# Up-projection of a feed-forward block on one core: 40 of 44 units issued from an explicit timetable, weight differences stored in half one and reloaded in half two

## Chip, cores and metric

One core of a Trainium2 chip. The metric is the device time of one execution of the whole kernel in microseconds, on the slowest core; here there is one. A lower time is better.

## The reference, cut to what matters

The kernel computes one layer of a streaming encoder, x of 2048 tokens x 1024, all in float32: three mixers (mLSTM, RG-LRU, Mamba-2), an output projection, and then a gated feed-forward block with a short causal convolution. The change lies in the first product of that block and what follows it up to the second one:

```
def causal_dwconv(x, w, b):             # K = 3 here
    ...
    for k in range(K):
        out = out + xp[:, k:k + S] * w[k]

def conv_ffn(x, w_up, conv_w, conv_b, w_down):
    u = causal_dwconv(x @ w_up, conv_w, conv_b)     # w_up: 1024 x 5632
    g, v = jnp.split(u, 2, axis=-1)
    return (jax.nn.gelu(g) * v) @ w_down            # w_down: 2816 x 1024

def reference(x, ...):
    ...
        h = rms_norm(x, norm_ffn_pre[l])
        x = x + rms_norm(conv_ffn(h, ...), norm_ffn_post[l])
```

## The kernel before, in words

**Units.** `phase_u` computes the up-projection, the convolution and the gate. It takes the tokens in two halves of 1024 and, in each, the 22 blocks of the feed-forward width (128 channels of the gate g and 128 of the value v): 44 units. Units 0 to 21 are the first half, 22 to 43 the second. Blocks come in pairs: block j, then block 11 + j. In the program's names `u0_14` is block 14 in the first half, and `uw0_15` the weights of block 15; the trace leaves the half and the running number out (`u_14`, `uw_15`). So block 4's unit comes after `u_14` and before `u_15`. "Unit 21" and the like mean the place in the order, counted from 0; "block 4's unit" goes by the name (its place is 8).

**A unit on PE.** A unit is a product [2 x 512 tokens, 1024] x [1024, 2 x 128], done by a Winograd form of 2 x 2 blocks: seven block products in place of eight. Each product is four k-steps (one 128-row slice each), and each k-step is three matmuls of 128 x 128 by 512 (lines 108 to 110: high times high part, high times low, low times high; `split3`), since float32 values are split in a high and a low part. That makes 84 matmuls. The products go b11 to bank X, b21 to Y, T4 to V, T1 to Z, T2 onto X, b22 onto Z, T3 onto X. Between them the banks' partial sums are copied out by ACT (line 356: `p1` of X, `p5` of Z, `u2` and `u3` of X), and DVE adds the copies and banks into the two outputs `ca` (gate channels) and `cb` (value channels) (lines 407, 421, 426, 427). X and Z take a further product after a copy, so that product can't begin before the copy is done.

**A unit's weights**, made in the unit before it (`Product.weights`): two raw tiles `ra`, `rb` are loaded on SP's queue, 512 KB each (four raw buffers in all). DVE makes four differences T1 to T4 (line 138). ACT makes the seven high parts (line 131, rounded copies), POOL the seven low parts (line 133, source minus high part).

**After the products** (`conv`, lines 430 to 447): ACT applies the last tap and the bias, DVE the other two taps for each output (line 438, `scalar_tensor_tensor`). The first two tokens of a half need two tokens of the half before: `ftail` holds them. In the first half DVE copies them there (line 446), in the second two tiny taps per output read them (line 442). ACT then does gelu on the gate channels (line 1740) and DVE the product of gelu and value (line 1741). For the down-projection, which is Winograd too, the block of a pair's first unit is kept, and after the second unit DVE makes four sums of blocks (lines 1634 to 1637). All blocks go to DRAM (`aS`, line 1619, on SP; for unit 42 on POOL's queue). Units 8, 11, 14 and 17 in order also make the sums of the second half's input, and units 20 to 41 one set of differences of the down weights each (lines 97 to 102: three on DVE, one on POOL).

**Ends.** Unit 0 finishes the phase before, unit 21 reloads PE's input blocks for the second half, unit 43 makes the first operands of the down-projection (`down_head`, `d_2l` at line 1785 is one of them). Units 21 and 22 take their products in another order (`sums_first`).

**What orders the work.** All of this is issued under a scheduler that places each engine's instructions by its own estimate of when operands are ready; `tc.high_priority(offset=EVAC)` pulls the copies and additions out of the banks forward.

## Time and profile before

| what | value |
|---|---|
| median of 3 runs | 2752.56 us (2748.34 to 2753.48) |
| profiled execution, its own time | 2752.25 us |
| its span | 2750.5 us |
| mean granted clock of PE | 0.961 |
| PE busy | 2490.6 us, 91% of the span |
| DVE busy | 2136.2 us, 78% |
| ACT busy | 1395.3 us, 51% |
| POOL busy | 1226.4 us, 45% |

The span is 1.75 us shorter than the execution's own time. It holds the mixers, the output projection, the up-projection from about 1270 to 2290 us, and the down-projection after it. Shares are means over all of these; a statement on the up-projection has to be read from its own stretch of time. Engines are named PE (matmuls), DVE, ACT, POOL and SP (issues most transfers). A PE that is shown busy runs at the granted clock: 1.00 is 2.4 GHz, 0.50 is 1.2 GHz.

### The profile page before, as it was taken

How to read it: one execution, taken by the hardware profiler on the slowest of the kernel's cores; microseconds unless marked ns; L12 is line 12 of the kernel's file. 1: busy time of each engine (PE TensorE's matmuls, PEld its weight loads, DVE VectorE, ACT ScalarE, POOL GpSimd, SP SyncE). 2: the span in 40 equal slices, each digit the busy share in tenths (PEclk: the TensorE clock that was granted, in tenths of full speed). 3: DMA queues.
4: the chain of work that ended last, by engine and by line, in shares of the span. 5: the costliest groups of instructions: out<-in, count | busy, mean ns of one | idle time of the engine just before them, and what ended most of it. 6: DMA issues, size and time to landing. Idle time of an engine off the chain costs nothing.

```text
span 2750.5 us, 38721 instructions
## 1 busy us (share of the span) xinstructions
PE 2490.6 (91%) x13658; PEld 2143.4 (78%) x13658; DVE 2136.2 (78%) x3055; ACT 1395.3 (51%) x2392; POOL 1226.4 (45%) x876
## 2 busy tenths in 40 slices
PE   8899989898888899999998989888989898999997
PEld 7677867688888778877776867666767677999997
DVE  5897689857888854556998889998989887557766
ACT  5456554544667765565444434543434356446343
POOL 5554454434344522224765556675555564003222
PEclk9999989999999999999999999999999999999999
DMA  7444633256666554665234333643434338767786
GB/s 244 149 145 144 221 127 118 83 178 184 167 174 179 180 183 146 206 217 172 95 119 139 122 123 111 191 149 119 138 127 138 126 121 304 252 202 267 265 267 206
DMA packets 290323, 467.41 MB, mean 170 GB/s; under 512 B 20832, under 2 KB 195680, under 8 KB 290128
## 3 DMA queue, kind: packets, MB, share of 16 engines
q1 hardware_dynamic: 289056, 461.53, 52.0%
q8 instruction: 107, 1.75, 0.3%
q0 software_dynamic: 784, 2.36, 0.2%
q10 hardware_dynamic: 288, 1.05, 0.1%
q14 instruction: 88, 0.72, 0.1%
HBM read 320.42 MB, written 144.44 MB: 169 GB/s over the span
## 4 chain that ended last, share of the span: by engine, by line
PE 22%; DVE 18%; DMA 8%; issue 5%; ACT 2%; POOL 1%; DVEq 0%; SPq 0%; ACTq 0%; POOLq 0%
PE mix L110 1%; PE mix L109 1%; PE mix L108 1%; PE e_7b L108 1%; PE e_7b L110 1%; PE e_7b L109 1%; DVE us L1634 1%; DMA e_0a<-aS 1%; PE e_2b L110 0%; PE e_2b L108 0%; PE e_2b L109 0%; PE e_6b L110 0%; PE e_6b L108 0%; PE e_6b L109 0%; DMA uw_9rb<-in_wup_u_dram 0%
## 5 line engine op out<-in xcount | busy, mean ns | idle before, releaser
L984 POOL TENSOR_TENSOR yn<-yn,yg 128x512 f32<-128x512 f32 x16 | 22.1, 1382 | 147.3 <-DMA yg<-gate 103.7
L1891 POOL TENSOR_TENSOR o<-o,y 128x512 f32<-128x512 f32 x14 | 24.6, 1757 | 125.7 <-DVE y L1890 25.9
L1785 POOL TENSOR_TENSOR d_0l<-d_0r,d_0h 128x768 fp32r<-128x768 f32 x2 | 3.9, 1942 | 146.8 <-ACT d_0h L1784 146.8
L108 PE MATMUL mix<-wo,ym 128*128 128x512 f32 x128 | 51.9, 405 | 1.6 <-DVE ysl L1015 1.6
L110 PE MATMUL mix<-wo,ym 128*128 128x512 f32 x128 | 51.0, 398 | 0.7 <-DVE ym L1015 0.7
L109 PE MATMUL mix<-wo,ym 128*128 128x512 f32 x128 | 50.6, 395 | 0.0
L109 PE MATMUL mix<-wol,ysh 128*128 128x512 f32 x128 | 50.2, 393 | 0.0
L110 PE MATMUL mix<-woh,ysl 128*128 128x512 f32 x128 | 50.1, 392 | 0.0
L108 PE MATMUL mix<-woh,ysh 128*128 128x512 f32 x128 | 49.7, 393 | 0.0
L1497 DVE TENSOR_TENSOR bh<-hT,g 128x512 f32<-128x512 f32 x32 | 20.7, 685 | 32.1 <-PE hT L1496 24.9
L1015 DVE TENSOR_TENSOR ym<-yT,ym 128x512 fp32r<-128x512 f32 x16 | 11.0, 689 | 35.6 <-ACT ym L1014 35.6
L986 DVE TENSOR_TENSOR yn<-yn,yg 128x1024 f32<-128x1024 f32 x16 | 21.2, 1328 | 18.7 <-ACT yg L985 18.7
L1801 DVE TENSOR_TENSOR e_10l<-e_10a,e_10h 128x896 fp32r<-128x896 f32 x15 | 16.3, 1090 | 23.8 <-ACT e_10h L1800 21.5
L1001 POOL TENSOR_SCALAR yrh<-yr 128x512 fp32r<-128x512 f32 x16 | 11.2, 702 | 51.7 <-DMA yr<-yrT 51.7
L1800 ACT ACTIVATE e_8h<-e_8a 128x896 fp32r<-128x896 f32 x15 | 14.3, 954 | 37.7 <-DMA e_8a<-aS 29.4
L616 DVE TENSOR_TENSOR hT<-xT,par 128x512 f32<-128x512 f32 x32 | 21.4, 683 | 14.7 <-PE xT L615 14.7
L615 PE MATMUL xT<-ident,x 128*128 128x128 f32 x128 | 20.2, 305 | 13.4 <-DVE x L609 8.3
L839 ACT ACTIVATE no<-n 128x256 f32<-128x256 f32 x64 | 23.9, 374 | 16.3 <-PE n L110 7.0
L1486 ACT ACTIVATE bt<-bx 128x1024 f32<-128x1024 f32 x16 | 16.9, 1059 | 27.7 <-DVE bx L1485 27.7
L1801 DVE TENSOR_TENSOR e_9l<-e_9a,e_9h 128x896 fp32r<-128x896 f32 x15 | 16.4, 1091 | 18.3 <-ACT e_9h L1800 16.7
L1801 DVE TENSOR_TENSOR e_6l<-e_6a,e_6h 128x896 fp32r<-128x896 f32 x15 | 23.9, 1590 | 8.0 <-ACT e_6h L1800 8.0
L985 ACT ACT_TABLE_LOAD x16 | 20.5, 1283 | 18.2 <-DMA yg<-gate 18.1
(9711 smaller groups left out, 11524.5 us busy)
## 6 DMA issues: line engine op xcount, KB each, us to landing
x<-in_x_dram SPq DMA_DIRECT2D x16, 512.0 KB, 6.5
hT<-hT SPq DMA_DIRECT2D x16, 512.0 KB, 3.9
gate<-no SPq DMA_DIRECT2D x64, 128.0 KB, 3.0
yn<-yns SPq DMA_DIRECT2D x16, 512.0 KB, 4.8
yg<-gate SPq DMA_DIRECT2D x16, 512.0 KB, 4.6
bx<-in_x_dram SPq DMA_DIRECT2D x16, 512.0 KB, 4.9
x<-bx SPq DMA_DIRECT2D x16, 512.0 KB, 2.8
h2T<-bh SPq DMA_DIRECT2D x16, 512.0 KB, 4.3
```

What stands on the lines that cost most here:

```text
L108: a = nc.tensor.matmul(pss, lh, rh, start=first, stop=False, skip_group_check=True)
L109: nc.tensor.matmul(pss, lh, rl, start=False, stop=False, skip_group_check=True)
L110: nc.tensor.matmul(pss, ll, rh, start=False, stop=last, skip_group_check=True)
L616: nc.vector.tensor_tensor(hT[:, 4 * q : 4 * q + 4], pt.rearrange("p (a b) -> p a b", a=4), col(par, "g1", 4 * q, 4).unsqueeze(2).to_broadc ...
L839: nc.scalar.activation(o, pt[:, 0:256], AF.Copy)
L984: nc.gpsimd.tensor_tensor(yn[:, 512:], yn[:, 512:], g[:, 512:], op=ALU.mult)
L985: nc.scalar.activation(g, g, AF.Sigmoid)
L986: nc.vector.tensor_tensor(yn, yn, g, op=ALU.mult)
L1497: nc.vector.tensor_tensor(hT[:, q * 4 : q * 4 + 4, :], pt.rearrange("p (a b) -> p a b", a=4), g2[:, 4 * q : 4 * q + 4].unsqueeze(2).to_bro ...
L1634: nc.vector.tensor_tensor(c, a11, a21, op=ALU.subtract)
L1801: nc.vector.tensor_tensor(al, a, ah.bitcast(F32), op=ALU.subtract)
L1891: nc.gpsimd.tensor_tensor(o[i][:, hs], o[i][:, hs], t, op=ALU.add)
```

## The change

Units 1 to 20 and 23 to 42 are written as events with a time each, in slots of one k-step (three matmuls), 28 slots a unit, and are then issued in the order of these times within `tc.manual_schedule()`. The four others (0, 21, 22, 43) stay with the scheduler. What is computed stays as it was. Beside the order, the code in the timetable differs in these points:

- The low parts are made by DVE (line 1911), all but one a unit (b11, on POOL).
- In the first half the four differences of each unit are stored in DRAM (`wT`, 4 x 256 KB a unit); in the second half they are loaded from there, seven slots before the end of the unit that stands two before theirs, and not made again.
- `ca` and `cb` have two more columns in front. In the second half ACT copies the tail into them, and each tap is one instruction; in the first half ACT instead of DVE saves the tails (line 1811).
- The taps of `cb` come ahead of those of `ca`.
- Unit 42's blocks are stored from SP's queue. The raw tiles of a unit are asked for two units ahead.

```
-        def weights(self, tp, w_ap, nm, sums_first=False, on_dve=()):
+        def weights(self, tp, w_ap, nm, sums_first=False, on_dve=(), diffs=None, save=None):
...
+            if diffs is not None:
+                T1, T2, T4 = (loaded(i) for i in (0, 1, 3))
+            else:
+                T1 = self.sub(nm + "T1", b12, b11)
...
+            if save is not None:
+                for i, t in enumerate((T1, T2, T3, T4)):
+                    nc.sync.dma_start(save[:, i], t)
...
+        def unit_events(n, at):
...
+            half, pos, b, nm = where(n)
+            t0, t1 = 28 * n, 28 * (n + 1)
...
+                for k in range(4):
+                    at(t0 + 4 * q + k, step, bk, wn, hn, first, k)
...
+            at(t0 + 4, keep, "p1", "X")
+            at(t0 + 9.4, c_of, 0)
+            at(t0 + 9.5, evac, "ca", 0, "Y", "p1")
+            at(t0 + 16, keep, "p5", "Z")
+            at(t0 + 20, keep, "u2", "X")
+            at(t0 + 24.1, c_of, 1)
+            at(t0 + 24.2, evac, "cb", 0, "Z", "u2")
+            at(t1, keep, "u3", "X")
+            at(t1, evac, "cb", 1, "X", "p5")
+            at(t1 + 0.8, evac, "ca", 1, "u3", "V", ALU.subtract)
...
+            at(t1 + 1.0, conv0, 1)
+            at(t1 + 2.8, conv0, 0)
+            if half == 0:
+                at(t1 + 4.6, tails)
+            at(t1 + 4.4, tap, 1, 1)
+            at(t1 + 6.3, tap, 1, 2)
+            at(t1 + 8.3, tap, 0, 1)
+            at(t1 + 10.2, tap, 0, 2)
+            at(t1 + 13, gelu)
+            at(t1 + 15.2, gate)
...
+            if b < NJ:
+                return [(17, keep)]
+            return [(17, store_blocks), (17.2, s3), (18.2, s1), (19.2, s2), (22, s4), (25, store_sums)]
+
+        def weight_events(n, at):
...
+            t0 = 28 * (n - 1)
...
+            at(t0 - 28 + (9 if aux(n - 3) else 2), load)
+            early = 5 if sums_first(n) else 0
+            if half:
+                at(t0 - 28 + 21, load_t)
+            else:
+                at(t0 + 1.7 - early, diff, "T1", "b12", "b11")
+                at(t0 + 2.4 - early, diff, "T2", "b22", "T1")
+                at(t0 + 3.1 - early, diff, "T4", "T2", "b21")
+                at(t0 + 12.2 - 2 * early, diff, "T3", "b22", "b12")
+                at(t0 + 5.1, store_t, 1, 2, 4)
+                at(t0 + 13.1, store_t, 3)
+            names = ("T1", "T2", "b22", "T3", "b11", "T4", "b21") if early else (
+                "b11", "b21", "T4", "T1", "T2", "b22", "T3"
+            )
+            for i, (name, th, tl) in enumerate(zip(
+                names, (-1, 2.5, 5, 7, 11, 15, 19), (0, 4.0, 6.2, 8.2, 12.1, 16.5, 20.2)
+            )):
+                at(t0 + th, hi, name)
+                at(t0 + tl, lo, name, nc.vector if i else nc.gpsimd)
...
+            at(t0 + 17.5, load)
+            at(t0 + 26, make)
+            at(t0 + 28 + 3, store)
...
+            with tc.manual_schedule():
+                for _, _, f, args in sorted(ev, key=lambda e: e[:2]):
+                    f(*args)
...
+        single(0, finish_b)
+        steady(1, NFF - 1)
+        single(NFF - 1, next_half)
+        single(NFF, None)
+        steady(NFF + 1, N - 1)
+        last(W_[N - 1], where(N - 1)[3], 1, where(N - 1)[2])
```

How the order of instructions moves, at three places. First ACT's queue in the first unit of block 4 (`u0_4`; the unit before it is `u0_14`, and `uw0_15` are the weights of the unit after it; `h` ends a high part, `p1`, `p5`, `u3` are copies out of banks, `v14` and `v36` the convolution's outputs). Before:

```order
L131 ACTIVATE uw0_15T4h_13797<-uw0_15T4_13795 128x512
L356 ACTIVATE u0_14u3_13744<-u0_14X_13648 128x512
L435 ACTIVATE u0_14v14_13748<-u0_14ca_13646,upar_12337 128x1024
L356 ACTIVATE u0_4p1_13837<-u0_4X_13821 128x512
L435 ACTIVATE u0_14v36_13753<-u0_14cb_13647,upar_12337 128x1024
L131 ACTIVATE uw0_15T1h_13801<-uw0_15T1_13791 128x512
L131 ACTIVATE uw0_15T2h_13805<-uw0_15T2_13793 128x512
L1740 ACTIVATE u0_14v14_13748<-u0_14v14_13748 128x1024
L131 ACTIVATE uw0_15b22h_13809<-uw0_15rb_13781 128x512
L131 ACTIVATE uw0_15T3h_13815<-uw0_15T3_13813 128x512
L356 ACTIVATE u0_4p5_13876<-u0_4Z_13823 128x512
```

and in the change:

```order
L1908 ACTIVATE uw0_15b21h_13815<-uw0_15ra_13650 128x512
L1801 ACTIVATE u0_14v14_13818<-u0_14ca_13705,upar_12337 128x1024
L1775 ACTIVATE u0_4p1_13829<-u0_4X_13793 128x512
L1811 ACTIVATE ftail_12339<-u0_14ca_13705 128x2
L1811 ACTIVATE ftail_12339<-u0_14cb_13776 128x2
L1908 ACTIVATE uw0_15T4h_13838<-uw0_15T4_13823 128x512
L1908 ACTIVATE uw0_15T1h_13852<-uw0_15T1_13804 128x512
L1908 ACTIVATE uw0_15T2h_13873<-uw0_15T2_13813 128x512
L1814 ACTIVATE u0_14v14_13818<-u0_14v14_13818 128x1024
L1908 ACTIVATE uw0_15b22h_13894<-uw0_15rb_13652 128x512
L1775 ACTIVATE u0_4p5_13901<-u0_4Z_13876 128x512
```

The convolution of `cb` (`v36`) moved ahead of that of `ca` (`v14`), the two copies of the tails came in (L1811), T3's high part moved from ahead of `p5` to behind it, and gelu (L1740 before, L1814 now) still stands ahead of `p5`.

Second, DVE's queue at the same place (`T1` to `T4` are weight differences; a name that ends in `l` is a low part). Before:

```order
L446 COPY ftail_12339<-u0_14cb_13647 128x2
L138 TENSOR_TENSOR uw0_5T1_13950<-uw0_5rb_13940,uw0_5ra_13938 128x512
L446 COPY ftail_12339<-u0_14ca_13646 128x2
L138 TENSOR_TENSOR uw0_5T2_13952<-uw0_5rb_13940,uw0_5T1_13950 128x512
L438 SCALAR_TENSOR_TENSOR u0_14v14_13748<-u0_14ca_13646,upar_12337,u0_14v14_13748 128x1023
L138 TENSOR_TENSOR uw0_5T4_13954<-uw0_5T2_13952,uw0_5ra_13938 128x512
L438 SCALAR_TENSOR_TENSOR u0_14v14_13748<-u0_14ca_13646,upar_12337,u0_14v14_13748 128x1022
L407 TENSOR_TENSOR u0_4ca_13819<-u0_4Y_13822,u0_4p1_13837 128x512
L438 SCALAR_TENSOR_TENSOR u0_14v36_13753<-u0_14cb_13647,upar_12337,u0_14v36_13753 128x1023
```

and in the change:

```order
L1785 TENSOR_TENSOR u0_14ca_13705<-u0_14u3_13790,u0_14V_13696 128x512
L138 TENSOR_TENSOR uw0_15T1_13804<-uw0_15rb_13652,uw0_15ra_13650 128x512
L138 TENSOR_TENSOR uw0_15T2_13813<-uw0_15rb_13652,uw0_15T1_13804 128x512
L138 TENSOR_TENSOR uw0_15T4_13823<-uw0_15T2_13813,uw0_15ra_13650 128x512
L1911 TENSOR_TENSOR uw0_15b21l_13816<-uw0_15ra_13650,uw0_15b21h_13815 128x512
L1743 SCALAR_TENSOR_TENSOR u0_14v36_13799<-u0_14cb_13776,upar_12337,u0_14v36_13799 128x1023
L1911 TENSOR_TENSOR uw0_15T4l_13839<-uw0_15T4_13823,uw0_15T4h_13838 128x512
L1743 SCALAR_TENSOR_TENSOR u0_14v36_13799<-u0_14cb_13776,upar_12337,u0_14v36_13799 128x1022
L1911 TENSOR_TENSOR uw0_15T1l_13853<-uw0_15T1_13804,uw0_15T1h_13852 128x512
L1743 SCALAR_TENSOR_TENSOR u0_14v14_13818<-u0_14ca_13705,upar_12337,u0_14v14_13818 128x1023
L1785 TENSOR_TENSOR u0_4ca_13864<-u0_4Y_13825,u0_4p1_13829 128x512
L1743 SCALAR_TENSOR_TENSOR u0_14v14_13818<-u0_14ca_13705,upar_12337,u0_14v14_13818 128x1022
```

Low parts (L1911) stand between the differences and the taps now, which were on another engine before; the copies of the tails (L446) are gone; the differences are those of the next unit (`uw0_15`), not of the one after (`uw0_5`); the taps of `v36` are ahead of those of `v14`.

Third, POOL's queue at the end of the stage (`aS` is the blocks' array in DRAM, `dl` and `d0_2l` are first operands of the down-projection). Before:

```order
L1608 TENSOR_TENSOR dl0_1_0_19909<-da0_1_19906,dh0_1_0_19908 128x384
L1619 DMA aS_9883<-u1_10v10_19755 128x4x128
L1608 TENSOR_TENSOR dl1_1_0_19919<-da1_1_19916,dh1_1_0_19918 128x384
L1619 DMA aS_9883<-us1_10_0_19978 128x2x128
L1619 DMA aS_9883<-u1_21v21_19770 128x2x256
L1619 DMA aS_9883<-us1_10_2_19989 128x2x128
L1619 DMA aS_9883<-u1_21v21_19770 128x2x256
L1619 DMA aS_9883<-u1_10v10_19755 128x2x128 x4
L1619 DMA aS_9883<-u1_21v21_19770 128x2x128
L1785 TENSOR_TENSOR d0_2l_20140<-d0_2r_20135,d0_2h_20139 128x768
```

and in the change:

```order
L1621 TENSOR_TENSOR dl0_1_0_19964<-da0_1_19961,dh0_1_0_19963 128x384
L1621 TENSOR_TENSOR dl1_1_0_19974<-da1_1_19971,dh1_1_0_19973 128x384
L1632 DMA aS_9883<-us1_10_0_20033 128x2x128
L1632 DMA aS_9883<-us1_10_2_20044 128x2x128
L2084 TENSOR_TENSOR d0_2l_20195<-d0_2r_20190,d0_2h_20194 128x768
L1632 DMA aS_9883<-u1_21v21_19825 128x2x256
```

Unit 42's store (the first row of `u1_10v10`) is gone from this queue, and `d0_2l`, which stood behind all the stores shown, has two of unit 43's ahead of it now; the others follow it.

## Rows read from the trace of the kernel before

**Rows 1.** Windows: first stretch, transition, second; last three columns: clock, DMA share, GB/s.

```profile
1290.00:1731.00 441.00, 404.36 (x1683) 326.37 (x1682) 388.15 (x370) 192.66 (x288) 270.40 (x149) 0.95 0.36 116
1731.00:1784.00 53.00, 41.32 (x169) 32.79 (x169) 50.68 (x51) 27.93 (x45) 35.48 (x21) 0.90 0.66 208
1784.00:2248.70 464.70, 410.66 (x1682) 329.97 (x1682) 410.80 (x438) 188.62 (x285) 263.23 (x164) 0.94 0.41 131
```

**Rows 2.** Timeline of PE (start, duration): first matmuls of blocks 4, 15, 6, 17.

```profile
1437.53 0.40 PE L108 MATMUL u_4X<-uQ_0a11h,uw_4b11h 128*128 128x512 f32 x1
...
1466.31 0.40 PE L108 MATMUL u_15X<-uQ_0a11h,uw_15b11h 128*128 128x512 f32 x1
...
1532.73 0.40 PE L108 MATMUL u_6X<-uQ_0a11h,uw_6b11h 128*128 128x512 f32 x1
...
1552.03 0.40 PE L108 MATMUL u_17X<-uQ_0a11h,uw_17b11h 128*128 128x512 f32 x1
```

**Rows 3.** PE's waits (us, times, longest): the first stretch's longest, the second's.

```profile
PE u_4Z L108 <- ACT u_4p L356: 7.5, 1, 7.5
...
PE u_5Z L108 <- ACT u_5p L356: 6.5, 1, 6.5
```

**Rows 4.** Windows before and behind the wait of block 4 (columns: rows 1).

```profile
1440.00:1451.00 11.00, 11.00 (x50) 8.94 (x49) 7.61 (x13) 5.02 (x7) 2.72 (x3) 1.00 0.71 239
...
1459.00:1462.20 3.20, 3.12 (x7) 2.48 (x8) 3.10 (x2) 1.03 (x3) 3.20 (x3) 0.50 0.39 145
```

**Rows 5.** Timeline of ACT, block 4's unit; in brackets the wait before.

```profile
1456.45 1.06 ACT L1740 ACTIVATE u_14v<-u_14v 128x1024 f32<-128x1024 f32 x1 [6.04 <-DVE u_14v L438]
...
1457.93 0.61 ACT L131 ACTIVATE uw_15T3h<-uw_15T 128x512 fp32r<-128x512 f32 x1
1458.45 0.58 ACT L356 ACTIVATE u_4p<-u_4Z 128x512 f32<-128x512 f32 x1
...
1466.88 0.58 ACT L356 ACTIVATE u_4u<-u_4X 128x512 f32<-128x512 f32 x1
```

**Rows 6.** Timeline of DVE, block 4's unit.

```profile
1449.90 0.69 DVE L138 TENSOR_TENSOR uw_5T<-uw_5rb,uw_5ra 128x512 f32<-128x512 f32 x1 [3.34 <-issue]
...
1452.28 2.28 DVE L438 SCALAR_TENSOR_TENSOR u_14v<-u_14ca,upar,u_14v 128x1023 f32<-128x1023 f32 x1
...
1455.09 1.27 DVE L438 SCALAR_TENSOR_TENSOR u_14v<-u_14ca,upar,u_14v 128x1022 f32<-128x1022 f32 x1
```

**Rows 7.** Windows of line 133 alone, first stretch (DVE, POOL, then clock, DMA, GB/s).

```profile
1290.00:1731.00 441.00, 1.77 (x1) 267.90 (x147) 0.95 0.36 116
```

**Rows 8.** Timeline of DVE in a place where POOL is still.

```profile
1904.92 0.68 DVE L138 TENSOR_TENSOR uw_14T<-uw_14rb,uw_14T 128x512 f32<-128x512 f32 x1
1905.63 0.69 DVE L138 TENSOR_TENSOR uw_14T<-uw_14T,uw_14ra 128x512 f32<-128x512 f32 x1
1906.24 0.68 DVE L138 TENSOR_TENSOR uw_14T<-uw_14rb 128x512 f32<-128x512 f32 x1
```

**Rows 9.** Windows of line 138 alone (DVE), first and second stretch.

```profile
1290.00:1731.00 441.00, 92.46 (x88) 0.95 0.36 116
1784.00:2248.70 464.70, 78.97 (x82) 0.94 0.41 131
```

**Rows 10.** Windows of line 442 alone (DVE, the tails' taps), second stretch.

```profile
1784.00:2248.70 464.70, 50.16 (x80) 0.94 0.41 131
```

**Rows 11.** DMA issues of the second stretch: KB each, median us to landing.

```profile
aS<-us SPq DMA_DIRECT2D x10, 256.0 KB, 2.3
...
p_4r<-in_wdn_dram SPq DMA_DIRECT2D x2, 512.0 KB, 6.4
...
p_8r<-in_wdn_dram SPq DMA_DIRECT2D x2, 512.0 KB, 3.6
```

**Rows 12.** PE's longest wait in the transition, then the one behind unit 42.

```profile
PE u_0Y L108 <- ACT u_0p L356: 7.8, 1, 7.8
...
PE e_0b L109 <- POOL d_2l L1785: 8.0, 1, 8.0
```

More of the change, by code (lines that the diff above doesn't have):

```diff
@@ new lines, in phase_u, with where, sums_first, prepare @@
+        N = NHALF * NFF
+        W_ = {0: w}
+        def where(n):
+            half, at = divmod(n, NFF)
+            return half, at, order[at], f"u{half}_{order[at]}"
+        def sums_first(n):
+            return n in (NFF - 1, NFF)
+        def prepare(n):
+            half, _, b, _ = where(n)
+            first = sums_first(n)
+            W_[n] = prod.weights(
+                uw, io["wup_u"][b], f"uw{half}_{b}", first, ("T4",) if first else (),
+                wT[b] if half else None, None if half else wT[b],
+            )
@@ new lines, in operand_steps, with view, keep, blocks @@
+        def operand_steps(half, b, st):
+            j = b % NJ
+            h = slice(0, 4)
+            def view(u):
+                return u.rearrange("p (u i t) -> p u i t", u=4, i=2)
+            def keep():
+                kept[j] = st["u", 0]
+                store_a(half, j, h, slice(0, 1), view(kept[j])[:, :, 0], nc.sync)
+            def blocks():
+                w, v = view(kept[j]), view(st["u", 0])
+                return w[:, :, 0], w[:, :, 1], v[:, :, 0], v[:, :, 1]
+            def store_blocks():
+                store_a(half, j, h, slice(1, 3), view(st["u", 0]).rearrange("p u i t -> p u (i t)"), nc.sync)
+            def s3():
+                a11, a21, _, _ = blocks()
+                st["c"] = rp.tile([P, 4, P], F32, name=f"us{half}_{j}", tag="T", bufs=prod.raws + 2)
+                nc.vector.tensor_tensor(st["c"], a11, a21, op=ALU.subtract)
+            def s1():
+                _, a21, _, a22 = blocks()
+                nc.vector.tensor_tensor(a21, a21, a22, op=ALU.add)
+            def s2():
+                a11, a21, _, _ = blocks()
+                nc.vector.tensor_tensor(a11, a21, a11, op=ALU.subtract)
+            def s4():
+                a11, _, a12, _ = blocks()
+                nc.vector.tensor_tensor(a12, a12, a11, op=ALU.subtract)
+            def store_sums():
+                a11, a21, a12, _ = blocks()
+                for i, q in enumerate((a21, a11, st["c"], a12)):
+                    store_a(half, j, h, slice(3 + i, 4 + i), q, nc.sync)
+            if b < NJ:
+                return [(17, keep)]
+            return [(17, store_blocks), (17.2, s3), (18.2, s1), (19.2, s2), (22, s4), (25, store_sums)]
@@ new lines, in steady, with at @@
+        def steady(first, end):
+            ev = []
+            def at(t, f, *args):
+                ev.append((t, len(ev), f, args))
+            for n in range(first, end):
+                unit_events(n, at)
+                if aux(n):
+                    aux_events(n, at)
+            for n in range(first + 1, end + 1):
+                weight_events(n, at)
+            with tc.manual_schedule():
+                for _, _, f, args in sorted(ev, key=lambda e: e[:2]):
+                    f(*args)
@@ new lines, in single @@
+        def single(n, after):
+            half, at, b, nm = where(n)
+            store = None
+            if aux(n):
+                store = prediffs(*aux(n)[1]) if aux(n)[0] == "diffs" else None
+            if n + 1 not in W_:
+                prepare(n + 1)
+            res = []
+            for c_, blk in zip(prod.unit(prod.hp, W_[n], nm, after, sums_first(n)), (b, NFF + b)):
+                res.append(
+                    conv(
+                        prod.hp, c_, [par[:, 3 * blk + k : 3 * blk + k + 1] for k in range(3)],
+                        par[:, 132 + blk : 133 + blk], ftail[:, blk, :], half, f"{nm}v{blk}", prod.cs,
+                    )
+                )
+            ug, uv = res
+            nc.scalar.activation(ug, ug, AF.Gelu_apprx_tanh)
+            nc.vector.tensor_tensor(ug, ug, uv, op=ALU.mult)
+            sums_ = operand(half, b, ug)
+            for st in (store, sums_):
+                if st is not None:
+                    st()
```

173 lines of the change are left out of this document (132 added, 41 removed).

## The prediction

> **What bounds the kernel now.** I read the stretches first, then the matmul starts, the waits of PE, and last the queue behind one wait. The up-projection is 44 units, and the 40 that the timetable takes over are two stretches, 441.0 us and 464.7 us [rows 1]: 905.7 us, 22.6 a unit. A unit without a wait needs less: in the first half, block 6's first matmul starts at 1532.73 and the next unit's at 1552.03, so 84 matmuls take 19.30 us, 0.230 each [rows 2]; 40 of them are 772 us. The reader is to see where the other 134 us are. Block 4's unit took 28.78 us [rows 2], 9.48 more, of which 7.5 is one wait [rows 3]; the rest, 1.9, is the clock: 1.00 of 2.4 GHz before the wait, 0.50 (1.2 GHz) for the 3 us behind it [rows 4]. In the first stretch 8 units have such a wait and in the second 10, nearly all for ACT's copy p5 (the long ones 5 to 7.5 us) [rows 3]. Bank Z has to be copied out before PE may add its next product to it. Why is the copy late? ACT had sat 6.04 us before gelu, waiting for DVE's taps; gelu stands ahead of p5 in its queue, and p5 started only at 1458.45 [rows 5]. DVE was late because it waited 3.34 us before a weight difference (raw tiles are handed back late, since POOL reads them slowly) and because its work is stretched: a tap took 2.28 us with POOL working and 1.27 without [rows 6]. DVE is busy 388 of 441 us and 411 of 464.7 [rows 1]. So the bound is a chain DVE, ACT, PE inside the unit; PE's own 19.3 us are the floor.
>
> **The change, part by part.** *Low parts from POOL to DVE.* Six of seven leave POOL. Before, POOL's 147 took 267.9 us [rows 7], 1.82 each; it keeps one a unit, and in the second half one difference of the down weights. DVE gains 6 x 0.61 = 3.7 us a unit (0.61: the distance of two independent 128x512 operations when POOL is still, 1905.63 to 1906.24; a dependent pair is 0.71 apart [rows 8]). What POOL gives back is larger: the 88 differences averaged 1.05 us [rows 9] instead of 0.61.
>
> *DVE's load after.* First half, per unit: 4 evacuations, 4 differences, 6 low parts and 2 operand sums (4 every second unit) are 16 x 0.61 = 9.8 us, and 3 dependent ones add 0.3; four taps 4 x 1.27 = 5.1; the product gate about 1.2, as a 1024-wide pass: 16.4 us. Second half: no differences (-2.7 with the 0.3) and three small ones of the down weights (+1.2): about 15. The tiny taps of the tails, 50.2 us for 80 [rows 10], go; ACT gets two small copies instead. Both loads fit into 19.3 us.
>
> *The chain to p5 in the new order.* From a unit's first matmul, u3's copy starts after 0.57 us (1466.31 to 1466.88) and takes about 0.58, as p5 does [rows 2, 5]. Then DVE does, in the printed order, two evacuations, three differences, three low parts, one more evacuation and four taps: 9 x 0.61 + 2 x 0.10 + 4 x 1.27 = 10.8 us. Gelu and b22's high part take 1.48 (1456.45 to 1457.93) and p5 0.58 [rows 5]. Sum: 0.57 + 0.58 + 10.8 + 1.48 + 0.58 = 14.0 us. PE wants bank Z after five products, 60 x 0.230 = 13.8. So the first half runs at its floor plus about 0.2: 19.5 us a unit, with no reserve: each microsecond of lateness goes into the unit. In the second half the three differences are gone and 2 us are spare: 19.4.
>
> *First half:* 20 x 19.5 = 390, plus 4 for filling the pipeline behind unit 0 and the four units that carry the extra sums: 394, against 441.0, so **-47**.
>
> *Second half:* 20 x 19.4 = 388, plus 7 because unit 23's weights are still made the old way inside unit 22 (its low parts on POOL): 395, against 464.7, so **-69.5**. The reload adds four loads of 256 KB a unit, 1.05 MB in 19.4 us, 54 GB/s. The same bytes as before in the shorter unit make 131 x 23.2 / 19.4 = 157 GB/s, so 211 in all; before the wait in block 4's unit 239 GB/s moved with the DMA engines 0.71 busy [rows 4], so there is room. Each difference is loaded seven slots, 4.8 us, before the next unit begins and read at least 3.5 us into it; transfers of 256 and 512 KB land in 2.3 and 3.6 us, 6.4 at worst [rows 11]. I take the reload as hidden; its cover is the 8 us, and what lies beyond is lost one for one.
>
> *Units 21 and 22* stay with the scheduler, 53.0 us now [rows 1], with a wait of 7.8 [rows 12]. Their loads are now queued on SP behind the store that waits for unit 20's gate, but POOL and DVE are freer. Bounds +8 and -8 (that wait more, or gone); I take **-2**.
>
> *End of the stage.* PE waits 8.0 us for POOL's d_2l [rows 12], which stood behind POOL stores waiting for DVE. The order now has it behind two of them only. Bounds 0 and -8; I take **-5**, since ACT makes its input not much earlier.
>
> *A rule against it.* DVE's busy share is the highest of the three helpers in both stretches, and the change puts work on it [rows 1]. The Trainium skill, Trace Analysis, Optimizing Scalar/DVE Operations, advises for a saturated DVE to give work to Scalar or even GPSIMD; this change does the reverse. By the rule this term would be a loss; it is the last rival below. By the rows it is a gain, because a DVE operation alone is 0.61 us and beside POOL 1.05 on average.
>
> **Sum.** The profiled execution took 2752.25 us (span 2750.5), the median of the runs is 2752.56, so nothing is lost between them. 2752.25 - 47 - 69.5 - 2 - 5 = 2628.75: **2629 us**.
>
> **The rivals.** *Better than that:* all 40 units at 19.3 (-133.7), transition and end at their better bounds (-16): 2603. For it: 0.2 us over the floor lies within the reading of the steps. Against: unit 23 has old-style weights.
>
> *The chain stays late.* Two places can do it. In the first half contention of POOL's last low part with the chain would add 1.0 us (2.28 - 1.27) a unit. In the second there is a loop: gate, store, load of down weights, their three differences, next unit's evacuation, taps, gate. Its parts are the store and load issues on SP about 1, the landing L, the differences 1.2, and from evacuation to gate 6 x 0.61 + 4 x 1.27 + gelu 1 + gate 1.2 = 10.9; with about 0.7 of hand-overs, 13.8 + L. With L = 3.6 it is 17.4 and hidden, with 6.4 it is 20.2 and bounds the unit. Against: the load is issued ahead of the four difference loads, not behind. At 20.2 to 21 us for all 40 units the stretches take 808 to 840, and with -7 for the rest it is 2648 to 2680.
>
> *No change:* the waits only move, say from p5 to u2 or to a weight part. The lookahead speaks against: every part is made a whole unit before PE reads it. 2747 to 2758.
>
> *Slower: the stretch is not POOL's doing.* If DVE's operations kept the mean durations of before, the six low parts would cost 6 x 1.05 = 6.3 us on a queue that is already busy 19.4 us a unit in the first half: 25.7, 514 us for 20 (+73). In the second half 20.5 - 2.5 [rows 10] - 3.9 [rows 9] + 6.3 = 20.4, with the idle 2.7 of now 23.1: 462 (-3). That is 2752 + 70 - 7 = 2815; it decides from a mean of 22.8 us a unit on. For it: the waits for raw tiles could stretch nothing but idle time. Against it: the same tap is 2.28 with a POOL operation beside it and 1.27 without [rows 6].
>
> **How the numbers follow.** Forecast 0.62 (its own range 2612 to 2645), better 0.10, chain late 0.22, no change 0.02, slower 0.04. The range 2600 to 2685 takes in the first three and most of the spread of their terms. 0.2% (5.5 us) is about what a measurement of this kernel can tell from no change: faster 0.94, same 0.02, slower 0.04.
>
> **What would show it.** Right: unit starts 19.3 to 19.6 us apart in both halves; no PE wait over 1.5 us among the 40 units and the clock at 1.00 throughout; low parts on DVE at 0.6 to 0.7 us, taps at 1.27; POOL below 60 us per stretch; DVE busy 80 to 85%. Wrong: units of 20 to 21 us with PE waiting for p5 in each (the chain), DVE waiting for the down weights' load (the loop), a first matmul waiting for a difference's low part (the reload), or taps still over 2 us (not POOL). A d_2l wait of 8 us would refute the end term.

## The result, and the profile after

The changed kernel takes **2672.47 us** (median of 4 runs, 2669.64 to 2676.08) against 2753.02 for the kernel before in the same comparison: a ratio of 0.9708 [0.9687, 0.9729], so 80.5 us less. Forecast were 123.6 less. The profiled execution took 2669.64 us, its span is 2667.9. The windows of the three stretches and of the 55 us behind them, which answer to [rows 1] (columns: stretch, us, PE, PEld, DVE, ACT and POOL busy, clock, DMA share, GB/s):

```profile
1279.90:1687.50 407.60, 392.81 (x1682) 317.91 (x1681) 349.19 (x443) 192.09 (x324) 40.68 (x28) 0.99 0.53 172
1687.50:1752.10 64.60, 47.94 (x169) 34.81 (x167) 58.82 (x61) 32.94 (x53) 36.58 (x23) 0.82 0.79 257
1752.10:2159.10 407.00, 394.80 (x1681) 316.08 (x1682) 319.69 (x393) 186.16 (x322) 55.56 (x46) 0.99 0.62 201
2159.10:2214.00 54.90, 39.54 (x211) 34.98 (x210) 42.28 (x51) 26.00 (x37) 35.52 (x25) 0.84 0.59 200
```

Read the lengths first. The first stretch fell from 441.0 to 407.6 us (-33.4), the second from 464.7 to 407.0 (-57.7), but the transition grew from 53.0 to 64.6 (+11.6), and from unit 43 to the end of the span it is 508.8 us in place of 501.8 (+7.0). The last 10.1 us of the span's difference (82.6) lie ahead of unit 1, where the two programs issue the same instructions but for the stores of unit 0's weight differences; over the profiles of this study the first matmul of unit 0 falls anywhere from 1253.0 to 1264.6 us, so they can't be put down to the change. DVE's busy time fell although it has more to do, and POOL's nearly went.

Fifteen of the 20 units of the first stretch take 19.31 us, the floor of [rows 2]. The five others take 28.1 (unit 1), 25.3, 20.9, 22.5 and 21.2. In the second stretch unit 23 takes 23.3, and then nearly every unit is a little long: 383.7 us for 19, 20.2 each. What PE waits for (us, times, longest), first stretch, then the start of the second and its longest, then the end:

```profile
PE u_11Z L108 <- ACT u_11p L1775: 3.5, 1, 3.5
PE u_15Z L108 <- ACT u_15p L1775: 3.0, 1, 3.0
PE u_18Z L108 <- ACT u_18p L1775: 2.9, 1, 2.9
...
PE u_11X L108 <- ACT uw_11b11h L131: 6.6, 1, 6.6
PE u_17Z L108 <- ACT u_17p L1775: 1.5, 1, 1.5
...
PE e_0b L109 <- POOL d_3l L2084: 10.0, 1, 10.0
```

It is still bank Z that waits for the copy p5, as in [rows 3], but the waits are shorter and sit elsewhere. Two places of DVE's timeline tell why. The first is the end of block 4's unit in the first half, one of the four with extra sums (x8; start, us, in brackets the idle time before and its releaser), with ACT's rows below it:

```profile
1443.32 0.69 DVE L1981 TENSOR_TENSOR x8c<-x8r 128x512 f32<-128x512 f32 x1 [0.35 <-DMA x8r<-h2T]
1445.32 0.69 DVE L1982 TENSOR_TENSOR x8r<-x8r,x8t 128x512 f32<-128x512 f32 x1 [1.30 <-DMA x8t<-h2T]
1446.04 0.69 DVE L1983 TENSOR_TENSOR x8r<-x8r 128x512 f32<-128x512 f32 x1
1446.77 0.69 DVE L1984 TENSOR_TENSOR x8t<-x8t,x8r 128x512 f32<-128x512 f32 x1
1447.38 0.68 DVE L1785 TENSOR_TENSOR u_4cb<-u_4X,u_4p 128x512 f32<-128x512 f32 x1
```

```profile
1457.98 1.06 ACT L1814 ACTIVATE u_4v<-u_4v 128x1024 f32<-128x1024 f32 x1 [4.76 <-DVE u_4v L1743]
...
1459.47 0.58 ACT L1775 ACTIVATE u_15p<-u_15Z 128x512 f32<-128x512 f32 x1
```

The extra sums stand ahead of the evacuation of `cb` and wait there for their load. PE was through with the unit at 1443.2, the evacuation came at 1447.38, and p5 was copied 12.7 us behind it (1460.05), as the order of the queue makes it: taps, gelu, p5. PE wanted it 13.8 us into the unit, at 1456.9.

The second place is block 4's unit in the second half: DVE, then SP, then POOL.

```profile
1908.28 1.23 DVE L1817 TENSOR_TENSOR u_14v<-u_14v,u_14v 128x1024 f32<-128x1024 f32 x1 [0.52 <-ACT u_14v L1814]
...
1914.85 0.42 DVE L99 TENSOR_TENSOR x30t<-x30r 128x256 f32<-128x256 f32 x1 [0.68 <-DMA x30r<-in_wdn_dram]
1915.31 0.84 DVE L101 TENSOR_TENSOR x30t<-x30r,x30t 128x256 f32<-128x256 f32 x1
1916.19 1.40 DVE L102 TENSOR_TENSOR x30t<-x30t,x30r 128x256 f32<-128x256 f32 x1
1917.51 0.68 DVE L1785 TENSOR_TENSOR u_4cb<-u_4X,u_4p 128x512 f32<-128x512 f32 x1
```

```profile
1909.53 0.38 SPq L1632 DMA_DIRECT2D aS<-u_14v  x1
1910.01 0.45 SPq L1957 DMA_DIRECT2D x30r<-in_wdn_dram  x1
1910.51 2.38 SPq L1894 DMA_DIRECT2D uw_5T<-wT  x4
```

```profile
1914.98 0.89 POOL L100 TENSOR_TENSOR x30t<-x30r 128x256 f32<-128x256 f32 x1 [18.16 <-DMA x30r<-in_wdn_dram]
1915.83 1.47 POOL L1911 TENSOR_TENSOR uw_5b11l<-uw_5ra,uw_5b11h 128x512 fp32r<-128x512 f32 x1
```

Here is the loop that the prediction had as a rival: gate (done at 1909.51), its store, the load of the down weights (issued at 1910.01, first used at 1914.85), their differences until 1917.5, and only then the evacuation that the next gate rests on. And the two operations that POOL has left fall just beside the differences: 0.84 and 1.40 us in place of 0.42. Averaged over units 25 to 41, the loop's parts are 12.5 us from the evacuation to the end of the gate, 0.5 to the issue of the load, 4.6 to the first difference and 2.7 to the next evacuation. That makes 20.3 us, for units of 20.2.

Unit 1, the longest of the first half, is late in another way. Unit 0 is still the scheduler's, and the low parts of unit 1's weights are made on POOL beside it. Three of unit 0's taps on DVE take 2.3 us each, unit 2's differences follow behind them, and their high parts stand ahead of p5, which ends 20.8 us into the unit (a tap of DVE, then p5 on ACT). No run tests this by itself.

```profile
1288.36 2.30 DVE L450 SCALAR_TENSOR_TENSOR u_0v<-u_0ca,upar,u_0v 128x1022 f32<-128x1022 f32 x1
```

```profile
1300.09 0.57 ACT L1775 ACTIVATE u_11p<-u_11Z 128x512 f32<-128x512 f32 x1
```

### The profile page after: what moved, and what is told of

It is laid out like the page before. It is cut to its first block, busy times and chain, and to the rows that moved or that the text cites. A ratio compares the mean times of both kernels' runs of the same rounds, so it can differ in the third digit from the quotient of the medians.

```text
span 2667.9 us, 38630 instructions
## 1 busy us (share of the span) xinstructions
PE 2469.9 (93%) x13658; PEld 2122.9 (80%) x13658; DVE 2015.5 (76%) x3086; ACT 1396.6 (52%) x2472; POOL 792.4 (30%) x636
## 3 DMA queue, kind: packets, MB, share of 16 engines
q10 hardware_dynamic: 288, 1.05, 0.1%
## 4 chain that ended last, share of the span: by engine, by line
PE 24%; DVE 13%; DMA 8%; issue 5%; ACT 4%; POOL 1%; SPq 0%; DVEq 0%; ACTq 0%; POOLq 0%
DMA e_10a<-aS 1%; PE e_4b L110 1%; PE mix L109 1%; PE mix L110 1%; PE mix L108 1%; PE e_4b L108 1%; PE e_7b L108 1%; PE e_4b L109 1%; PE e_7b L109 1%; PE e_7b L110 1%; DVE e_6l L2100 1%; PE e_3b L110 1%; PE e_3b L108 0%; PE e_3b L109 0%; PE e_2b L110 0%
## 5 line engine op out<-in xcount | busy, mean ns | idle before, releaser
L996 POOL TENSOR_TENSOR yn<-yn,yg 128x512 f32<-128x512 f32 x16 | 21.6, 1352 | 145.1 <-DMA yg<-gate 103.5
L1509 DVE TENSOR_TENSOR bh<-hT,g 128x512 f32<-128x512 f32 x32 | 20.7, 686 | 34.0 <-PE hT L1508 34.0
L627 PE MATMUL xT<-ident,x 128*128 128x128 f32 x128 | 20.4, 306 | 12.5 <-DVE x L621 8.4
L628 DVE TENSOR_TENSOR hT<-xT,par 128x512 f32<-128x512 f32 x32 | 21.4, 683 | 13.6 <-PE xT L627 13.6
L1270 DVE SCALAR_TENSOR_TENSOR s_1L<-s_1A,gt,nmask 128x128 f32<-128x128 f32 x64 | 29.2, 482 | 1.0 <-PE s_1pp L1330 0.9
L2100 DVE TENSOR_TENSOR e_5l<-e_5a,e_5h 128x896 fp32r<-128x896 f32 x15 | 23.9, 1596 | 7.4 <-ACT e_5h L2099 7.3
```

The costliest lines, as they stand in the source:

```text
L627: nc.tensor.transpose(pt[:, j * P : (j + 1) * P], xt[:, k * P : (k + 1) * P], ident)
L628: nc.vector.tensor_tensor(hT[:, 4 * q : 4 * q + 4], pt.rearrange("p (a b) -> p a b", a=4), col(par, "g1", 4 * q, 4).unsqueeze(2).to_broadc ...
L996: nc.gpsimd.tensor_tensor(yn[:, 512:], yn[:, 512:], g[:, 512:], op=ALU.mult)
L1270: nc.vector.scalar_tensor_tensor(L[j][:, hd, :], A[:, hd, j, :], ga[:, hd, 2 * g0 + j : 2 * g0 + j + 1], nmask, op0=ALU.subtract, op1=ALU.add,
L1509: nc.vector.tensor_tensor(hT[:, q * 4 : q * 4 + 4, :], pt.rearrange("p (a b) -> p a b", a=4), g2[:, 4 * q : 4 * q + 4].unsqueeze(2).to_bro ...
L2100: nc.vector.tensor_tensor(al, a, ah.bitcast(F32), op=ALU.subtract)
```

## The experiments

Each stretch below is measured from the first matmul of its first unit to that of the next stretch, in the profile of that kernel. Ratios are against the kernel before, run with it (2749.74 to 2754.54 us).

| kernel | median us | ratio [95%] | first | transition | second |
|---|---|---|---|---|---|
| before | 2752.56 | 1 | 441.0 | 53.0 | 464.7 |
| changed | 2672.47 | 0.9708 [0.9687, 0.9729] | 407.6 | 64.6 | 407.0 |
| lo_on_pool | 2712.57 | 0.9861 [0.9841, 0.9880] | 446.2 | 68.5 | 402.9 |
| before_lo_dve | 2646.57 | 0.9627 [0.9607, 0.9647] | 388.6 | 47.2 | 412.4 |
| reload_only | 2729.49 | 0.9927 [0.9913, 0.9942] | 436.2 | 53.0 | 446.1 |
| all_scheduled | 2636.73 | 0.9593 [0.9577, 0.9609] | 387.3 | 46.2 | 413.0 |
| no_reload | 2679.03 | 0.9737 [0.9718, 0.9756] | 406.2 | 61.8 | 412.6 |
| p5_first | 2660.01 | 0.9655 [0.9627, 0.9683] | 398.4 | 65.4 | 404.1 |
| late_sums | 2672.69 | 0.9707 [0.9688, 0.9727] | 412.4 | 67.3 | 398.3 |
| p5_late_sums2 | 2648.45 | 0.9629 [0.9613, 0.9645] | 403.4 | 65.7 | 387.2 |
| unit20_single | 2664.16 | 0.9686 [0.9665, 0.9708] | 407.8 | 53.5 | 411.2 |
| end_on_sp | 2676.25 | 0.9727 [0.9708, 0.9745] | 410.7 | 64.5 | 406.3 |
| hybrid | 2607.27 | 0.9482 [0.9468, 0.9496] | 387.2 | 46.2 | 389.6 |
| hybrid_no_reload | 2638.67 | 0.9580 [0.9560, 0.9601] | 388.5 | 46.2 | 405.9 |

### What each part gives: low parts, order, reload

**lo_on_pool**

```
-                at(t0 + tl, lo, name, nc.vector if i else nc.gpsimd)
+                at(t0 + tl, lo, name, nc.gpsimd)
```

> Edit: the timetable's low parts all go to POOL at the same slots, as before the change; order and all else stay. Theory A (DVE operations are stretched by POOL's, and the move of the low parts is what gave the gain): DVE's evacuations and differences average about 1.05 us and taps about 2 again, p5 comes some 3 to 4 us late in each unit, units 22 to 23.5 us, 2672 plus about 96 (60 to 130), 2730 to 2800 us. Theory C (the written order gave the gain, the engine does not matter; DVE even has 3.7 us a unit less to do): taps at 1.3, units 19.3 to 20.4, 2652 to 2675 us.

The time lies between the ranges of the two theories, because each half follows another one. In the first the written order without the move gains nothing (446.2 us); units without extra sums take 21.0, less than theory A had. The taps of the first half alone (line 1743: DVE busy, clock, DMA share, GB/s), with the low parts on POOL and in the changed kernel:

```profile
1279.20:1725.40 446.20, 140.82 (x76) 0.97 0.49 158
```

```profile
1279.90:1687.50 407.60, 97.08 (x76) 0.99 0.53 172
```

That is 1.85 us a tap beside POOL and 1.28 without. In the second half the taps are stretched as much (141.29 us for 76), and yet the stretch is 402.9, no longer than in the changed kernel: in this order the low parts' move is worth nothing there. The loop holds that half here too, and its parts are nearly the same: 12.3, 0.5, 4.6 and 2.7 us. DVE's taps take longer in it, but DVE has no low parts to do between them.

**before_lo_dve**, the move alone, in the scheduler's order:

```
             def ent(n, src):
-                eng = nc.vector if n in on_dve else nc.gpsimd
+                eng = nc.gpsimd if n == "b11" and self.wp1 is None and self.ws == 20 and nm[0] == "u" else (nc.vector if nm[0] == "u" else (nc.vector if n in on_dve else nc.gpsimd))
```

(The test of `nm` keeps the other products' weights on their engines. The move covers all 44 units; the changed kernel makes it in the 40 of the timetable.)

> Edit: the kernel before, with the low parts of the up-projection's weights on DVE but b11's; no timetable, no reload. lo_on_pool showed that the timetable without this move gains nothing in the first half (446.2 us against 441.1). Theory A (in the first half the move is the gain, in the second the order): first stretch 405 to 420, second 450 to 465; about 2715 us. Theory C (the move gains only with the written order): first stretch 435 or more, 2740 us or more; DVE, at 388 of 441 us before, takes 81 us more and becomes the bound.

It gains more than either theory had it, in both halves, and more than the whole change: 103.5 us (from the 2750.06 of its own comparison) against 80.5. Its windows of the two stretches:

```profile
1283.00:1671.60 388.60, 387.88 (x1684) 316.46 (x1683) 356.56 (x495) 195.16 (x289) 59.68 (x22) 1.00 0.43 130
...
1718.80:2131.20 412.40, 396.55 (x1682) 316.97 (x1682) 360.32 (x567) 188.17 (x281) 57.95 (x40) 0.99 0.47 151
```

PE is busy 387.88 of 388.60 us at full clock: the first stretch is at its floor. DVE took over all low parts but one a unit and is busy 357 us where it was 388 [rows 1].

**reload_only**, the changed kernel's weights (store and reload of the differences) in the scheduler's order, with the low parts on POOL: every unit is issued as `single`, no timetable. Unit 42's blocks are stored from SP's queue here and in all_scheduled, as in the changed kernel.

> Edit: the kernel before with the reload alone: all in the scheduler's order, low parts on POOL, no timetable. Theory A (in the second half either way of unloading DVE helps, since it is busy 411 of 465 us; the first half needs the move of the low parts): first stretch 441 as before (within 5), second from 464.5 to 425 to 445; 2712 to 2732 us. Theory I (POOL's stretching of DVE alone sets the second half): second 455 or more, 2743 us or more.

The second stretch fell by 18.6 us to 446.1, a microsecond short of the range; 20 us in all against its own comparison's 2749.74. Alone, the reload gives far less than the move alone. What the written order gives without both was not run, nor were the smaller parts of the change by themselves (the two columns for the tails, `cb`'s taps first, raw tiles asked for earlier).

**all_scheduled**, the same with the low parts on DVE as in before_lo_dve.

> Edit: the changed kernel without any timetable: all units in the scheduler's order, low parts on DVE but b11's (as in before_lo_dve), differences stored in the first half and reloaded in the second. Against before_lo_dve it has the reload alone. Theory A (in before_lo_dve every second unit of the second half waits 1 to 2.3 us for T4's high part, whose difference comes late from a busy DVE): the reload takes 82 differences from DVE, these waits go, second stretch from 412.3 to 392 to 400; about 2630 us. Theory H (the reloads queue on SP behind stores that wait for DVE, so the wait stays): second stretch 412 or more, 2646 us or more.

Theory A fell: the second stretch is 413.0, as without the reload (412.4). The waits for T4's high part are gone and waits for p5 of up to 2.5 us stand in their place. The 9.8 us that it is below before_lo_dve do not come from there: the profiles show 6.9 of them behind unit 43, and the two intervals overlap.

**no_reload**, in the timetable:

```
-            if half:
-                at(t0 - 28 + 21, load_t)
-            else:
+            if True:
...
-                at(t0 + 5.1, store_t, 1, 2, 4)
-                at(t0 + 13.1, store_t, 3)
```

(The scheduler's units get the same: nothing saved, nothing loaded.)

> Edit: the differences of the weights are made on DVE in the second half as in the first, at the same slots; nothing of them is stored or loaded. Theory A (loop): three differences stand between the evacuation and the taps, 2.1 us more in the loop, and the load of the down weights lands about 1.2 us sooner without four loads behind it: 20.4 to 21.3 us a unit, second stretch about 425, first stretch as before, about 2690 us. Theory D (the reload is neutral: DVE has room for 2.7 us a unit): 2672 within 5. Theory E (its traffic, 54 GB/s more, costs more than it saves): second stretch 395 or less, 2660 us or less.

The second stretch is 5.6 us longer, in the direction of theory A at a third of its size; on the time the intervals overlap. So within this timetable the reload is worth little.

### What holds the timetable above its floor

**p5_first**

```
-            at(t1 + 13, gelu)
-            at(t1 + 15.2, gate)
+            at(t1 + 16.2, gelu)
+            at(t1 + 16.4, gate)
```

> Edit: in the timetable gelu and the gate move from slots 13 and 15.2 to 16.2 and 16.4, so that ACT copies p5 ahead of gelu; nothing else. Theory A (two limits: in the first half p5 waits behind gelu, in the second a loop gate, store, load of down weights, their differences, next evacuations, taps, gelu, gate of 20.4 us): the waits after the four units with extra sums (6.0, 1.6, 3.2 and 1.9 us) shrink to 1 us or less each, first stretch 407.6 to about 397; the second stretch stays at 407 (within 3), since the loop does not pass through p5, and PE's wait only moves to another copy. About 2661 us. Theory B (p5 behind gelu is the limit in both halves): the second stretch falls too, by some 18 us to 389: about 2643 us.

Theory A held: the first stretch is 398.4 (the units behind extra sums 20.7, 19.3, 20.6 and 19.3), the second 404.1, within the 3 us, with PE's waits there moved from p5 to u2.

**late_sums**

```
-            at(t0 - 28 + (9 if aux(n - 3) else 2), load)
+            at(t0 - 28 + (9 if aux(n - 3) else 2), load)
+            at(t0 - 28 + (15.6 if aux(n - 3) else 2), load_b)
...
-            at(t0 + 26, make)
-            at(t0 + 28 + 3, store)
+            at(t0 + 28 + 13, make)
+            at(t0 + 28 + 15.5, store)
```

(`load` now loads `ra` alone, `load_b` loads `rb`.)

> Edit: as p5_late_sums2, but gelu and the gate at their places in the changed kernel, ahead of p5. Theory A (the loop through the load of the down weights, not ACT's order, holds the second half): second stretch 387 to 393 as in p5_late_sums2; 2650 to 2660 us. Theory B (p5 behind gelu holds it): second stretch 400 or more, 2664 us or more.

Neither: 398.3. Behind unit 23, eleven units are at 19.3 to 19.5, the other eight, each second one, at 19.6 to 20.8, waiting for p5 again: those that follow a unit in which DVE makes the operand sums. With the loop gone, p5 behind gelu still holds these.

**p5_late_sums2**, both edits. A first form, p5_late_sums, loaded both raw tiles at slot 9 as before; it gave no time, since its instructions wait for each other in a circle (a deadlock). Hence the later load of `rb`.

> Edit: as p5_first, and the differences of the down weights (and the extra sums of the first half) are made at slot 13 of the next unit instead of slot 26, their store at 15.5 instead of 3, and the second raw tile of weights is then loaded at slot 15.6 instead of 9, because its buffer is free only there; the load of the down weights stays at 17.5, so that it has some 16 us instead of 6. Theory A (the loop through that load bounds the second half): second stretch from 404 to 388, units 19.4 apart, no DVE wait for the load; first stretch about 395; about 2641 us. Theory B (something else holds the second half at 20.2 us a unit): not faster than p5_first (2660), second stretch within 3 us of that one's.

The second stretch is 387.2 us, PE at full clock and busy for all but 0.6 us of it:

```profile
1755.00:2142.20 387.20, 386.57 (x1681) 315.38 (x1682) 317.71 (x397) 193.74 (x326) 70.32 (x46) 1.00 0.63 209
```

and the same differences of the down weights, now off the loop, take 0.41 to 0.43 us and wait for no load:

```profile
1902.96 0.41 DVE L99 TENSOR_TENSOR x29t<-x29r 128x256 f32<-128x256 f32 x1
1903.40 0.43 DVE L101 TENSOR_TENSOR x29t<-x29r,x29t 128x256 f32<-128x256 f32 x1
1903.87 0.42 DVE L102 TENSOR_TENSOR x29t<-x29t,x29r 128x256 f32<-128x256 f32 x1
```

So the second half had two limits close to each other, the loop and p5 behind gelu. Taking p5 from behind gelu alone gave 2.9 us, taking the loop apart alone 8.7, both 19.8. The first half is 5 us above p5_first's: the extra sums now stand among the taps, and two units are 3.9 us long. In late_sums, too, the first half did not become shorter (412.4). The total is 7 us above what was expected.

### Transition and end

**unit20_single**

```
-        steady(1, NFF - 1)
+        steady(1, NFF - 2)
+        single(NFF - 2, None)
```

> Edit: the first timetable ends before unit 20, which goes back to the scheduler with units 21 and 22. Theory A (the transition is 11.7 us longer than before because the loads of the second half's blocks may start only behind unit 20's stores on SP): the transition shrinks from 64.7 to 53 to 57 us, unit 20 costs up to 2 more: 2662 to 2667 us. Theory G (unit 23's weights, queued behind the store of unit 21's sums, and the reloads are what is late): transition 62 us or more, 2670 us or more.

The transition is 53.5 us, as before the change. In the changed kernel SP issues the first load of the second half's sums (`uS_0s1r`) 12.2 us into unit 21, behind unit 20's stores and unit 22's weights, and the weights of unit 23 behind the stores of unit 21's sums:

```profile
1692.15 0.43 SPq L269 DMA_DIRECT2D uw_0ra<-in_wup_u_dram  x1
...
1699.69 0.33 SPq L216 DMA_DIRECT2D uS_0s1r<-summed  x1
...
1738.23 1.57 SPq L1632 DMA_DIRECT2D aS<-u_10v  x2
...
1743.57 0.42 SPq L269 DMA_DIRECT2D uw_11ra<-in_wup_u_dram  x1
```

With unit 20 in the scheduler's hands that load goes out 3.5 us into unit 21 (1689.7), and unit 22's raw tiles were asked for at 1668.1 and 1673.2, around the start of unit 20 (1670.4) and not in unit 21:

```profile
1690.86 2.29 SPq L287 DMA_DIRECT2D uw_0T<-wT  x4
1693.25 0.38 SPq L216 DMA_DIRECT2D uS_0s1r<-summed  x1
```

The 8.3 us of the medians are less than the 11.1 of the stretch, and their intervals overlap; the second stretch is 4.2 us longer than in the changed kernel.

**end_on_sp**

```
-                operand(half, b, u[0], slice(2 * h, 2 * h + 2), nc.gpsimd)()
+                operand(half, b, u[0], slice(2 * h, 2 * h + 2), nc.sync)()
```

> Edit: unit 43's blocks are stored from SP's queue instead of POOL's. Theory A (after the change these stores stand behind d_2l on POOL, and DVE's last sums and so d_3l wait for them): PE's wait of 10.0 us for d_3l falls below 3, the tail (from unit 43 to the last matmul) from 500 to about 490; about 2663 us. Theory F (POOL's own work, 6.2 us for d_2l, is what is late): tail 498 or more, 2670 us or more.

PE no longer waits for d_3l, as theory A had it; but it waits 5.5 us for d_2l instead, which POOL takes 7.20 us for, and the time did not move: the numbers are those of theory F. What happens in the changed kernel can be read from DVE and POOL at the end:

```profile
2194.54 1.08 DVE L2100 TENSOR_TENSOR e_3l<-e_3a,e_3h 128x896 fp32r<-128x896 f32 x1
2201.78 0.43 DVE L1650 TENSOR_TENSOR u_21v<-u_21v,u_10v 128x256 f32<-128x256 f32 x1 [6.16 <-DMA aS<-u_21v]
...
2206.82 0.43 DVE L1650 TENSOR_TENSOR u_21v<-u_21v,u_10v 128x256 f32<-128x256 f32 x1 [3.61 <-DMA aS<-u_21v]
2207.16 1.22 DVE L2086 TENSOR_TENSOR d_3l<-d_3T,d_3h 128x1024 fp32r<-128x1024 f32 x1
```

```profile
2191.10 6.19 POOL L2084 TENSOR_TENSOR d_2l<-d_2r,d_2h 128x768 fp32r<-128x768 f32 x1 [1.72 <-ACT d_2h L2085]
2197.23 0.73 POOL L1632 DMA_DIRECT2D aS<-u_21v  x1
...
2207.85 2.18 POOL L2084 TENSOR_TENSOR d_3l<-d_3r,d_3h 128x768 fp32r<-128x768 f32 x1
```

d_2l went ahead of the stores; so the stores of `u_21v` are late, DVE's last sums (line 1650) overwrite what these read and wait for them, 6.16 and 3.61 us, and d_3l waits behind both. Why d_2l itself took 6.19 us stands in the last section. What the end needs to become shorter than before was not found; it is 493 to 504 us from unit 43 to the last matmul in all these profiles.

### A better version

**hybrid**: units 0 to 22 in the scheduler's order with the low parts on DVE, units 23 to 42 in the timetable of p5_late_sums2.

```
-        steady(1, NFF - 1)
+        for n in range(1, NFF - 1):
+            single(n, None)
         single(NFF - 1, next_half)
         single(NFF, None)
         steady(NFF + 1, N - 1)
```

(The low parts' edit is that of all_scheduled, the timetable's those of p5_late_sums2.)

> Edit: units 0 to 22 in the scheduler's order with the low parts on DVE, differences stored; units 23 to 42 in the timetable of p5_late_sums2. Theory A (the pieces add up: the scheduler's first half and transition, the timetable's second half): first stretch 388 to 391, transition 47 to 50, second 387 to 390, 2646.6 - 25 = about 2622 us. Theory J (a seam between the two costs, as at unit 1 with 28.1 us): transition and first unit 8 to 15 us longer, 2630 to 2637 us.

**2607.27 us**, 0.9482 [0.9468, 0.9496]: 65 us below the changed kernel by the medians. The pieces add up, without a seam, and the time is 15 us below their expected sum. Against before_lo_dve the profiles show 22.8 us in the second stretch and 6.6 behind unit 43; why the latter is so was not tested.

```profile
1281.20:1668.40 387.20, 386.72 (x1681) 315.27 (x1680) 358.63 (x494) 195.81 (x288) 45.46 (x23) 1.00 0.62 196
...
1714.60:2104.20 389.60, 388.51 (x1680) 316.40 (x1681) 320.54 (x409) 194.38 (x326) 59.75 (x40) 1.00 0.64 212
```

**hybrid_no_reload**, with no_reload's edits on top:

> Edit: as hybrid, but the differences of the weights are made on DVE in the second half at the first half's slots, and nothing of them is stored or loaded. Theory A (with the loop gone, DVE's 15 us a unit leave room for 2.7 us of differences and 0.3 of dependent steps under the 19.3 of PE): second stretch 387 to 392, 2607 us within 6. Theory K (DVE is too full with them): units of 20 us and more, second stretch 400 or more, 2618 us or more.

Theory K: 405.9. Unit 23 takes 33.7 us in place of 22.8, and of the others every second one 19.4 to 20.8. Here the reload is worth the 16 us of this stretch, 10.9 of them in unit 23 alone; the medians say 31, of which the profiles show 5 ahead of unit 0 and 6 behind unit 43, where its part is open.

## Why the prediction was right, and where it was not

The direction, the whole range (2600 to 2685) and the mechanism of the first half held. The forecast itself and its own range (2612 to 2645) did not: the gain is two thirds of the one forecast, and the time is in the slow part of the second case ("the chain stays late", 2648 to 2680). There was some luck in it: 10.1 of the 82.6 us between the two profiles lie ahead of unit 1, where the prediction saw no gain.

- **The low parts and their stretch of DVE: right.** Low parts take 0.68 us on DVE (81.24 for 120, the row below), taps 1.28, POOL is busy 41 and 56 us. lo_on_pool shows cause and effect, and the rival "slower" fell with it: DVE's durations are POOL's doing. Two readings on the way were loose. The 1.05 us of a difference is a mean duration, whose counterpart without POOL is 0.68 and not the 0.61 from start to start. And POOL's slow reading as the reason of the 3.34 us in [rows 6] is not shown: the view names no releaser there, and SP issued the load of that raw tile at 1444.65 only, behind stores of the extra sums that it issued until 1443.7.

```profile
1279.90:1687.50 407.60, 81.24 (x120) 29.41 (x20) 0.99 0.53 172
```

- **The credit was shared out wrongly.** The prediction let the move of the low parts and the order work together in both halves. In the first half the order with the reload gains nothing and the move alone 52.4 us; in the second each gains about as much as both together (61.8 with the order and the reload, 52.3 with the move, 57.7 with all).
- **First half, -47 forecast, -33.4 measured.** The 14.0 us to p5 held: it ends 13.3 to 13.6 us into the fifteen units that are at 19.31. The mis-sized term is the 4 us for filling and the extra sums: unit 1 took 8.8 over the floor and the four units behind extra sums 12.7, 21.5 in all. "With no reserve: each microsecond of lateness goes into the unit" was written there, but not applied to the extra sums, which put off block 4's evacuation by 4.1 us (1443.32 to 1447.38), 1.3 of them a wait for a load. What gave this half 9.2 us back is p5 ahead of gelu (398.4); to take the sums from ahead of the evacuation did not (403.4 with both).
- **Second half, -69.5 forecast, -57.7 measured.** The reload was hidden, as taken. What failed is the choice against the loop, on the ground that the load of the down weights is issued ahead of the four others. It is, and still landed 4.8 us after its issue in the rows above, and the differences took 2.7 us for the 1.2 put in, because POOL's rest falls beside them. By the prediction's own sum, 13.8 us and the landing, these two make 20.1 us a unit, for 20.2 measured; unit 23 (23.3) cost 3 us less than put in. p5_late_sums2 shows loop and p5 as the limits.
- **Units 21 and 22, -2 forecast, +11.6 measured**, beyond the bound of +8. The prediction saw the loads queued behind a store on SP and priced it at a wait of PE; what moved is the start of all of the half's loads. unit20_single gives it back.
- **The end, -5 forecast, +7.0 in the profiles.** The order was read right (d_2l behind two stores only), but not what came behind: the stores that d_2l passed, and DVE's sums that wait for these. PE's wait of 8.0 us for d_2l became 1.9 for d_2l and 10.0 for d_3l, so the gain did not come. The 7.0 us as a loss are not shown: from unit 43 to the end of the span it is 509.9 us in before_lo_dve, whose end has the order of before, and 502.0 in late_sums, whose end has that of the change.
- **The page's rule.** DVE was the busiest helper, and the Trainium skill, Perfetto Trace Analysis, Optimizing Scalar/DVE Operations, says that taking work off a saturated DVE, to Scalar or even GPSIMD, may make sense. The prediction left out what the same paragraph adds: between GPSIMD and DVE it might not help, since the two share an SBUF read port. The trace agrees with that reservation: giving DVE work of POOL lowered DVE's busy time from 388 to 357 us in before_lo_dve.

## What to carry to other kernels

Before writing an order by hand, try the one engine move in the old order: here that alone was worth more than the move, the timetable and the reload together, and the timetable paid only where it was kept to the half in which it helps. A queue written by hand needs its reserve where the engines meet: copies that free a bank go ahead of long work that can wait, and work that hangs on a load goes where it holds up no evacuation, as in the second half here. When an operation is let pass others in a queue, look at who waits for those that it passed.
